# Where a kernel forms the sums of its weight blocks: the down projection's sums move from the input projection to the merge

## The chip, the cores and the metric

The kernel runs on one core of a Trainium2 chip. The metric is the device time of one execution in microseconds (us), the median of several runs. The profile comes from one further execution, recorded by the hardware profiler.

The engines are named as in the profile: PE is the matrix engine (PEld its weight loads), DVE the vector engine, ACT the scalar engine, POOL the GpSimd engine, SP the engine that does nothing but issue transfers (DMAs). SP, ACT and POOL each issue transfers in the order of their own instruction list; an issue that has to wait holds up the issues listed after it.

## The reference

One layer of a streaming encoder over 2048 + 64 = 2112 rows of width 1024, in float32:

- `proj = rmsnorm(x) @ w_in` with 5376 columns. From its parts come a gated causal convolution (branch A), an RWKV-7 recurrence over time with an 8-head matrix state (branch B) and 2048 gate columns.
- `m = sigmoid(gA) * (A @ w_conv_out) + sigmoid(gB) * (B @ w_rwkv_out)`, then `x += rmsnorm(m @ w_o)`. This is the merge.
- `x += rmsnorm((silu(h @ w_up_a) * (h @ w_up_b)) @ w_down)` with `h = rmsnorm(x)` and an inner width of 2816. These are the up and the down projection.

## The kernel before

**Stages.** Three follow one another. The input projection (`phase_a`) takes 160 weight blocks of 128 columns; each block is multiplied with two blocks of 264 rows, and one such product is a half unit, so that there are 320 half units. Three generators for the recurrence (`scan_prep`, `scan_solve`, `scan_chain`) are advanced between them. The merge (`merges`) goes three times, each time for two blocks of 352 rows, through `merge` (products with `w_ab`, gates multiplied in on DVE) and `merge_out` (products with `w_o`). The feed-forward stage (`ffn`) goes three times through the up and the down projection.

**Products.** A float32 operand is split into a high part (ACT) and a low part (DVE), and each product is three matmuls.

**Sums of weights.** The feed-forward products use a Strassen-like scheme of seven products of half-size blocks in place of eight. It needs four sums of the 2 x 2 blocks of each weight matrix. The kernel forms them itself: `weight_sums` loads the four blocks of a job into tiles named `sw` (four buffers), makes four additions on DVE in place (S_1, S_3, S_2, S_4) and writes the four results to scratch in memory, `us_s` for the up and `ds_s` for the down projection. There are 22 jobs for up (blocks of 128 x 512) and 12 for down (128 x 512, and 128 x 384 for every third). A job has four steps: loads; two additions; two additions; stores. Loads and stores are issued by SP. `sum_step` is called once per half unit and takes a step from half unit 24 on, every second time (`SUM_STEP = 2`): 136 steps. What is then left is written at the end of `projections`.

**Background work of the merge.** `self.bg` is a list of generators; `tick` advances each by one step. `merge` ticks twice after each of its 16 iterations, `merge_out` 16 times in all (32 in the third round), so there are 48, 48 and 64 ticks. In the list are the loads of the next round's operands (`merge_load`), the residual with its norm (`residual`, which adds on DVE into a tile `r`, stores it as `x1_s` from POOL, and loads the next one) and in the third round `norm_first`.

**Order.** The kernel gives each instruction a place in the written order only. The compiler's framework then lists the instructions of each engine in an order of its own, in which written order is a priority: an instruction whose operands and buffers are free can come long before its written place. Waits follow from the buffers: a load into a buffer waits until everything that used the buffer's last content is finished.

Of the kernel before, what the change touches and what calls it, by code (L numbers as in the profile page):

```python
# [9 lines left out]
F32 = mybir.dt.float32  # L10
# [3 lines left out]
ALU = mybir.AluOpType  # L14
AX = mybir.AxisListType

P = 128
# [12 lines left out]
NF = DFF // P  # L30
# [18 lines left out]
FB = T // 6  # L49
FH = NF // 2  # L50
HK = KT // 2
# [2 lines left out]

S_1, S_2, S_3, S_4 = range(4)

SUM_STEP = 2

DOWN = (("B11", "X", True), ("T2", "Y", False), ("B21", "X", False), ("D", "Y", False), ("T1", "Z", True), ("T4", "Y", False), ("B22", "Z", False))
UP = ("B11", "T1", "T2", "B21", "D", "B22", "T4")  # L60
# [4 lines left out]
KCHUNKS = ((0, 4), (4, 4), (8, 3))  # L65
# [20 lines left out]
class Trunk:  # L86
# [174 lines left out]
    def phase_a_setup(self, pool):  # L261
        nc = self.nc
        self.pa = pool
        self.pr_hist = pool.tile([P, 14], F32, name="pr_hist", bufs=1)
        nc.vector.memset(self.pr_hist, 0.0)
        self.u_hist = pool.tile([P, 4, 2], F32, name="u_hist", bufs=1)
        nc.vector.memset(self.u_hist, 0.0)
        self.pr_hist_s = pool.tile([P, 14], F32, name="pr_hist_s", bufs=1)
        nc.scalar.dma_start(out=self.pr_hist_s, in_=self.i["state_shift"])
        self.u_hist_s = pool.tile([P, 4, 2], F32, name="u_hist_s", bufs=1)  # L270
        nc.scalar.dma_start(out=self.u_hist_s, in_=self.i["state_conv"])
        self.hbufs, self.nb = 17, NB
        self.napply = self.sadd = nc.vector
        self.sq = "hf", 2
        self.later, self.parts, self.side = [], 0, []
        self.ready = 0
        self.summing, self.sum_wait = self.weight_sums(), 24
        self.lora_in, self.conv_u, self.kf, self.bn = {}, {}, {}, {}

    def project(self, w, h, n):  # L280
# [303 lines left out]
        for _ in self.summing:  # L584
            pass

    def weight_sums(self):

        nc = self.nc
        up, wd = self.i["w_up"], self.i["w_down"]  # L590
        jobs = [(lambda i, j, f=f: up[NF * i + f, :, HK * j:HK * j + HK, :], lambda s, f=f: self.us_s[s, f]) for f in range(NF)]
        for u in range(4):
            for k0, kn in KCHUNKS:
                jobs.append((lambda i, j, u=u, k0=k0, kn=kn: wd[2 * u + i, :, FH * j + k0:FH * j + k0 + kn, :],
                             lambda s, u=u, k0=k0, kn=kn: self.ds_s[s, u, :, k0 * P:(k0 + kn) * P]))
        for src, dst in jobs:
            w = {}
            for i in range(2):
                for j in range(2):
                    x = src(i, j)  # L600
                    w[i, j] = self.pa.tile([P, HK, P], F32, name="sw", bufs=4)[:, :x.shape[1]]
                    nc.sync.dma_start(out=w[i, j], in_=x)
            yield
            for n, (x, y) in enumerate((((1, 1), (1, 0)), ((1, 0), (0, 0)), ((0, 0), (1, 1)), ((0, 1), (0, 0)))):
                nc.vector.tensor_tensor(out=w[x], in0=w[x], in1=w[y], op=ALU.add)  # L605
                if n % 2:
                    yield
            for k, sm in (((1, 1), S_1), ((1, 0), S_3), ((0, 0), S_2), ((0, 1), S_4)):
                nc.sync.dma_start(out=dst(sm), in_=w[k].rearrange("p k c -> p (k c)"))
            yield  # L610

    def sum_step(self):
        self.sum_wait -= 1
        if self.sum_wait <= 0:
            self.sum_wait = SUM_STEP
            next(self.summing, None)
# [748 lines left out]
    def merges(self, th):  # L1365

        src, merged, last = [], [], []
        first = self.merge_load(0, src)
        next(first)
        self.fill(2)  # L1370
        for _ in first:
            pass
        self.fill()
        self.gates = self.gate_loads()
        self.gates_in = []
        for q in range(3):
            if q == 2:
                self.bg.append(self.norm_first(th, merged, last))
            ms = self.merge(q, src)
            src = []  # L1380
            if q < 2:
                self.bg.append(self.merge_load(q + 1, src))
            else:
                merged.append(True)
            self.bg.append(self.merge_out(q, ms))
        last.append(True)
# [98 lines left out]
```

## Time and profile before

| | |
|---|---|
| median of three runs | 3300.65 us (3297.57 to 3308.23) |
| profiled execution | 3302.73 us, span from first to last instruction 3301.0 us |
| mean granted PE clock | 0.975 of full speed |
| input projection | 0 to about 1510 us of the span |
| merge | about 1510 to 1900 us |
| feed-forward | about 1900 us to the end |
| DVE additions on `sw` | 136, the first at 24.7 us, the last at 1149.8 us |

A profile row of a group of instructions reads: line, engine, operation, destination <- source, shapes, count; then busy time and mean of one in ns; then the idle time of the engine before them and what ended it. PE is busy for 95% of the span, but a matmul at half the clock counts as busy too, so the granted clock has to be read beside it.

### The profile page before, as it was taken

To read this page: it belongs to the slowest core of one execution; us is meant where nothing else is said; L and a number is where in the kernel's file an instruction comes from. 1 tells how busy PE (TensorE), PEld (TensorE's weight loads), DVE (VectorE), ACT (ScalarE), POOL (GpSimd) and SP (SyncE) were. 2 spreads that over 40 slices of the span, in tenths; PEclk is the share of its full clock that TensorE was granted. 3 is DMA by queue.
4 is the path that set the end of the run, shared out by engine and by line. 5 is a ranking of instruction groups with operands and counts; after the bars stand their busy time and mean duration, and the time that the engine had idled before them with its cause. 6 is when DMAs were issued, how large, how long until landed. Compare 5 with 4: busy or idle time off the path is not lost.

```text
span 3301.0 us, 64364 instructions
## 1 busy us (share of the span) xinstructions
PE 3138.5 (95%) x23060; PEld 3061.5 (93%) x23060; DVE 2370.1 (72%) x5091; ACT 1734.6 (53%) x3418; POOL 493.7 (15%) x906
## 2 busy tenths in 40 slices
PE   6999999999989999998999999999999999999997
PEld 5889899889989999998999999999999999999997
DVE  6766777778778867655476877776767776766667
ACT  6534664564476445544434455556645466544464
POOL 2310123122014200000010011210011200111100
PEclk9999899999989999999999999999999999999999
DMA  8778767775676756546475467778767877766675
GB/s 267 244 246 246 231 197 235 224 221 168 208 223 184 218 159 176 140 146 227 131 225 159 152 209 240 241 244 263 234 214 229 266 246 237 235 191 189 189 253 167
DMA packets 526226, 699.53 MB, mean 212 GB/s; under 512 B 111136, under 2 KB 358496, under 8 KB 525904
## 3 DMA queue, kind: packets, MB, share of 16 engines
q1 hardware_dynamic: 468528, 592.67, 59.0%
q0 software_dynamic: 25456, 72.20, 5.9%
q10 hardware_dynamic: 31920, 30.54, 2.7%
q8 instruction: 181, 2.97, 0.4%
q14 instruction: 141, 1.16, 0.1%
HBM read 522.10 MB, written 173.12 MB: 211 GB/s over the span
## 4 chain that ended last, share of the span: by engine, by line
issue 42%; PE 23%; DVE 7%; POOL 5%; DMA 4%; ACT 2%; POOLq 0%; SPq 0%; ACTq 0%; DVEq 0%
PE mm L136 18%; POOL tp_s L1228 3%; PE pu L136 3%; PE gy L136 1%; DVE w_lo L150 1%; DVE ti L761 1%; POOL x_s L1087 1%; DVE tm L759 1%; POOL out_y L1087 1%; DMA w_raw<-in_w_in 1%; DMA x<-x_s 1%; DMA lo_s<-ks 0%; PE tr L140 0%; POOL nb_s L1172 0%; PE pa L136 0%
## 5 line engine op out<-in xcount | busy, mean ns | idle before, releaser
L136 PE MATMUL mm<-h_hi,w_hi 128*128 128x264 f32 (+1 forms) x5112 | 1591.9, 312 | 52.0 <-DVE f L1247 22.0
L136 PE MATMUL mm<-h_hi,w_lo 128*128 128x264 f32 (+1 forms) x5112 | 1564.8, 306 | 9.3 <-DVE w_lo L150 6.0
L136 PE MATMUL mm<-h_lo,w_hi 128*128 128x264 f32 (+1 forms) x5112 | 1566.1, 307 | 6.0 <-DVE h_lo L217 5.3
L136 PEld LDWEIGHTS mm<-h_hi,w_hi 128*128 128x128 f32 x5112 | 979.1, 192 | 77.3 <-DVE f L1247 25.9
L136 PEld LDWEIGHTS mm<-h_hi,w_lo 128*128 128x128 f32 x5112 | 980.2, 192 | 12.2 <-DVE w_lo L150 7.4
L136 PEld LDWEIGHTS mm<-h_lo,w_hi 128*128 128x128 f32 x5112 | 980.4, 192 | 11.0 <-DVE h_lo L217 6.7
L188 ACT CAST w_hi<-w_raw 128x512 fp32r<-128x512 f32 (+1 forms) x810 | 488.0, 608 | 537.4 <-PE mm L136 318.7
L189 DVE TENSOR_TENSOR w_lo<-w_raw,w_hi 128x512 fp32r<-128x512 f32 (+1 forms) x810 | 539.6, 673 | 259.9 <-ACT w_hi L188 253.2
L136 PE MATMUL mm<-t_hi,w_hi 128*128 128x352 f32 x1116 | 360.9, 323 | 1.0 <-ACT mm L1329 1.0
L136 PE MATMUL mm<-t_hi,w_lo 128*128 128x352 f32 x1116 | 358.2, 321 | 0.0
L136 PE MATMUL mm<-t_lo,w_hi 128*128 128x352 f32 x1116 | 358.1, 321 | 0.0
L150 DVE TENSOR_TENSOR w_lo<-w_raw,w_hi 128x1024 fp32r<-128x1024 f32 x168 | 206.0, 1227 | 106.8 <-ACT w_hi L149 98.2
L149 ACT CAST w_hi<-w_raw 128x1024 fp32r<-128x1024 f32 x168 | 175.9, 1048 | 141.9 <-PE mm L136 95.7
L1228 POOL DMA_DIRECT2D tp_s<-f x231 | 125.1, 542 | 578.7 <-DVE f L1247 339.7
L136 PEld LDWEIGHTS mm<-t_hi,w_hi 128*128 128x128 f32 x1116 | 209.4, 188 | 1.9 <-ACT mm L1329 1.5
L136 PEld LDWEIGHTS mm<-t_lo,w_hi 128*128 128x128 f32 x1116 | 209.8, 188 | 0.3
L136 PEld LDWEIGHTS mm<-t_hi,w_lo 128*128 128x128 f32 x1116 | 209.6, 188 | 0.0
L189 DVE TENSOR_TENSOR t_lo<-d,t_hi 128x352 fp32r<-128x352 f32 x198 | 97.1, 521 | 73.6 <-ACT t_hi L188 73.0
L188 ACT CAST t_hi<-d 128x352 fp32r<-128x352 f32 x198 | 91.3, 486 | 89.6 <-DMA d<-tp_s 82.7
L759 DVE TENSOR_TENSOR tm<-al,ti 128x60 f32<-128x60 f32 (+27 forms) x527 | 117.9, 224 | 8.9 <-DMA gt_s<-psv 1.1
L761 DVE TENSOR_TENSOR ti<-ti,tm 128x60 f32<-128x60 f32 (+27 forms) x527 | 117.6, 223 | 7.7
L605 DVE TENSOR_TENSOR sw<-sw 128x512 f32<-128x512 f32 (+1 forms) x136 | 93.4, 687 | 34.1 <-DMA sw<-in_w_up 29.5
(207 smaller groups left out, 3753.6 us busy)
## 6 DMA issues: line engine op xcount, KB each, us to landing
w_raw<-in_w_in SPq DMA_DIRECT2D x168, 512.0 KB, 4.3
w_raw<-us_s SPq DMA_DIRECT2D x264, 256.0 KB, 3.2
w_raw<-in_w_up SPq DMA_DIRECT2D x198, 256.0 KB, 3.1
tp_s<-f POOLq DMA_DIRECT2D x231, 176.0 KB, 3.6
d<-tp_s SPq DMA_DIRECT2D x105, 352.0 KB, 3.9
w_raw<-ds_s SPq DMA_DIRECT2D x96, 256.0 KB, 3.6
sw<-in_w_up SPq DMA_DIRECT2D x88, 256.0 KB, 4.6
us_s<-sw SPq DMA_DIRECT2D x88, 256.0 KB, 3.4
```

What stands on the lines that cost most here:

```text
L136: self.nc.tensor.matmul(out, lhsT, rhs, **kw)
L149: nc.scalar.copy(out=hi[:, :kt], in_=raw[:, :kt])
L150: nc.vector.tensor_tensor(out=lo[:, :kt], in0=raw[:, :kt], in1=hi[:, :kt].bitcast(F32), op=ALU.subtract)
L188: nc.scalar.copy(out=hi, in_=x)
L189: (eng or nc.vector).tensor_tensor(out=lo, in0=x, in1=hi.bitcast(F32), op=ALU.subtract)
L605: nc.vector.tensor_tensor(out=w[x], in0=w[x], in1=w[y], op=ALU.add)
L759: nc.vector.tensor_tensor(out=tv, in0=al[0:np_, u, u + 1:32].unsqueeze(1).broadcast_to([np_, k, m]), in1=ti[0:np_, 0:k, u:u + 1].broadcast ...
L761: nc.vector.tensor_tensor(out=tu, in0=tu, in1=tv, op=ALU.add)
L1087: (nc.sync if rows else nc.gpsimd).dma_start(out=dst[d, :, t0:t0 + n], in_=x)
L1228: nc.gpsimd.dma_start(out=self.tp_s[TP[op], i], in_=x)
```

## The change

The sums of the up projection begin at half unit 72 instead of 24 and take a step every third half unit, so one job in 12 half units (88 steps). The sums of the down projection leave the input projection. They become a background generator of the merge, put into `self.bg` before its first round: 24 jobs of at most two blocks of 128 columns for each of the four loads (128 x 256, and 128 x 128 for every sixth), 96 steps. They live in the tiles named `d` (two buffers, each with room for two blocks), which are otherwise used only by the down projection's operands. Their loads stay on SP; their stores are issued by POOL. For both, the loads are now issued in the order in which the additions use them.

```
-SUM_STEP = 2
+SUM_FIRST, SUM_STEP = 72, 3
+ADDS = (((1, 1), (1, 0), S_1), ((1, 0), (0, 0), S_3), ((0, 0), (1, 1), S_2), ((0, 1), (0, 0), S_4))
...
-        self.summing, self.sum_wait = self.weight_sums(), 24
+        self.summing, self.sum_wait = self.up_sums(), SUM_FIRST
...
+    def sums_of(self, load, queue, src, dst):
+        nc = self.nc
+        w = load(src)
+        yield
+        for n, (x, y, _) in enumerate(ADDS):
+            nc.vector.tensor_tensor(out=w[x], in0=w[x], in1=w[y], op=ALU.add)
+            if n % 2:
+                yield
+        for x, _, sm in ADDS:
+            queue.dma_start(out=dst(sm), in_=w[x])
+        yield
+    def up_sums(self):
+        up = self.i["w_up"]
+        def load(src):
+            w = {}
+            for i, j in ((1, 1), (1, 0), (0, 0), (0, 1)):
+                w[i, j] = self.pa.tile([P, HK, P], F32, name="sw", bufs=4)
+                self.nc.sync.dma_start(out=w[i, j], in_=src(i, j))
+            return w
+        for f in range(NF):
+            yield from self.sums_of(load, self.nc.sync, lambda i, j: up[NF * i + f, :, HK * j:HK * j + HK, :],
+                                    lambda s: self.us_s[s, f].rearrange("p (k c) -> p k c", c=P))
+    def down_sums(self):
+        wd = self.i["w_down"]
+        def load(src):
+            w = {}
+            for i in (1, 0):
+                t = self.bc.tile([P, 2, FB], F32, name="d", bufs=2)
                 for j in range(2):
                     x = src(i, j)
+                    w[i, j] = t[:, j, :x.shape[1] * P].rearrange("p (k c) -> p k c", c=P)
+                    self.nc.sync.dma_start(out=w[i, j], in_=x)
+            return w
+        for u in range(4):
+            for k0 in range(0, FH, 2):
+                k1 = min(k0 + 2, FH)
+                yield from self.sums_of(load, self.nc.gpsimd, lambda i, j: wd[2 * u + i, :, FH * j + k0:FH * j + k1, :],
+                                        lambda s: self.ds_s[s, u].rearrange("p (k c) -> p k c", c=P)[:, k0:k1, :])
...
         self.fill()
+        self.bg.append(self.down_sums())
         self.gates = self.gate_loads()
```

## Rows read from the trace of the kernel before

**Rows 1.** Busy time by stage: PE, PEld, DVE, ACT, POOL, PEclk, DMA share, GB/s.
```profile
0.00:600.00 600.00, 532.61 (x4399) 510.13 (x4400) 429.98 (x935) 316.89 (x614) 129.25 (x232) 0.94 0.75 237
600.00:1180.00 580.00, 551.56 (x4990) 525.18 (x4988) 470.94 (x1252) 334.12 (x672) 135.71 (x264) 0.96 0.68 204
1180.00:1510.00 330.00, 323.63 (x3021) 311.51 (x3019) 209.25 (x557) 167.56 (x288) 23.16 (x32) 1.00 0.52 151
1510.00:1582.00 72.00, 63.83 (x370) 61.91 (x371) 50.72 (x98) 28.55 (x58) 2.44 (x3) 0.91 0.81 263
1582.00:1643.00 61.00, 61.00 (x385) 61.00 (x385) 27.62 (x50) 29.95 (x63) 0.00 (x0) 1.00 0.41 129
1643.00:1710.00 67.00, 64.96 (x392) 63.96 (x391) 51.45 (x100) 18.32 (x34) 8.40 (x16) 0.97 0.62 190
1710.00:1775.00 65.00, 64.74 (x404) 64.21 (x403) 33.58 (x64) 32.53 (x70) 0.28 (x1) 1.00 0.50 162
1775.00:1842.00 67.00, 60.93 (x354) 58.59 (x353) 58.16 (x109) 22.70 (x46) 8.66 (x16) 0.96 0.71 219
```

**Rows 2.** SP's issues in the first 40 us: start us, duration us, instruction.
```profile
5.88 0.34 SPq L602 DMA_DIRECT2D sw<-in_w_up  x1
34.91 2.26 SPq L602 DMA_DIRECT2D sw<-in_w_up  x4
```

**Rows 3.** Weight blocks of the input projection split on ACT (L149), by window.
```profile
0.00:100.00 100.00, 9.40 (x9) 0.93 0.81 265
100.00:200.00 100.00, 15.68 (x15) 0.97 0.81 257
```

**Rows 4.** DVE groups, 600 to 1180 us, shapes apart: the additions of the down sums.
```profile
L605 DVE TENSOR_TENSOR sw<-sw 128x512 f32<-128x512 f32 x32 | 22.9, 716 | 0.1
L605 DVE TENSOR_TENSOR sw<-sw 128x384 f32<-128x384 f32 x16 | 9.9, 619 | 0.0
```

**Rows 5.** The chain that ended last, 600 to 1200 us: start us, us, what.
```profile
611.92 0.60 DVE sw L605
...
677.20 5.93 DMA ds_s<-sw
...
1133.92 1.57 DVE sw L605
```

**Rows 6.** Waits of SP, 600 to 1180 us: total us, times, longest.
```profile
SPq L602 <- DMA ds_s<-sw: 22.3, 15, 4.8
```

**Rows 7.** Waits of PE, 600 to 1180 us.
```profile
PE pa L136 <- DVE v L704: 10.9, 6, 2.4
...
PE mm L136 <- DVE sw L605: 3.2, 1, 3.2
```

**Rows 8.** Waits of DVE for the sums' loads, whole input projection.
```profile
DVE sw L605 <- DMA sw<-in_w_up: 29.5, 12, 5.6
```

**Rows 9.** DVE groups, 1510 to 1842 us: an addition of width 352.
```profile
L1033 DVE TENSOR_TENSOR f<-f,mm 128x352 f32<-128x352 f32 x44 | 22.6, 514 | 4.2 <-PE mm L136 3.5 <-DMA f<-gt_s 0.7
```

**Rows 10.** The chain in the second merge: one residual tile from addition to the next addition.
```profile
1656.54 0.45 DVE r L1086
1656.98 0.30 issue
1657.29 0.55 POOL x_s L1087
1657.83 0.91 issue
1658.75 3.52 DMA x_s<-r
1662.29 2.30 DMA r<-in_x
1664.61 0.05 DVEq L1086
```

**Rows 11.** Tile `r`, 1510 to 1900 us: its loads (first and last start), and DVE's wait.
```profile
L1072 SPq DMA_DIRECT2D r<-in_x x34: 327/333/934, 1557.8 to 1842.6; - x34
...
DMA r<-in_x: 17.2, 21
```

**Rows 12.** Waits of PE in the merge, 1510 to 1842 us.
```profile
PE mm L136 <- DVE f L1033: 5.0, 5, 1.9
```

More of the change, by code (lines that the diff above doesn't have):

```diff
@@ L585, in projections @@
             pass
-    def weight_sums(self):
+    def sums_of(self, load, queue, src, dst):
         nc = self.nc
[L590 to L596, printed above, removed]
-            w = {}
-            for i in range(2):
+        w = load(src)
[7 more added lines that the diff above has]
+        yield
@@ L599, in weight_sums @@
+    def down_sums(self):
[4 more added lines that the diff above has]
+                t = self.bc.tile([P, 2, FB], F32, name="d", bufs=2)
                 for j in range(2):
                     x = src(i, j)
[L601 to L607, printed above, removed]
@@ L608, in weight_sums @@
-            for k, sm in (((1, 1), S_1), ((1, 0), S_3), ((0, 0), S_2), ((0, 1), S_4)):
-                nc.sync.dma_start(out=dst(sm), in_=w[k].rearrange("p k c -> p (k c)"))
-            yield
+                    w[i, j] = t[:, j, :x.shape[1] * P].rearrange("p (k c) -> p k c", c=P)
[6 more added lines that the diff above has]
+                                        lambda s: self.ds_s[s, u].rearrange("p (k c) -> p k c", c=P)[:, k0:k1, :])
```

## The prediction

> **What bounds the kernel now.** I read the busy time by stage first, with the granted clock beside it, then the waits of PE and the chain that ended last inside the stages that the change touches. PE bounds every stage: in the three rounds of the merge that the change fills (1510 to 1775 us) it is busy for 61.0 of 61 us in one and 64.7 of 65 in another [rows 1]. What can be gained or lost is therefore PE's idle time and the time at a lower clock. From 600 to 1180 us, where the down sums run, PE is idle for 580 - 551.6 = 28.4 us and its clock averages 0.96, which is another 0.04 x 580 = 23 us of work time. From 1180 to 1510, with no sums, 6.4 us are idle in 330 and the clock is 1.00; but that stretch also has less recurrence work, so the difference is not the sums' alone [rows 1]. DVE, at 470.9 of 580 us, is the engine behind most waits: the two largest in which DVE releases PE are shown, and one of them, 3.2 us, is an addition of the sums itself [rows 7].
>
> The second thing to see is that written places do not bind. The sums are written from half unit 24 on. Two halves make a block, so that is after the twelfth block of the main loop and the two in front of it; only 9 blocks were split in the first 100 us and 15 in the next [rows 3], which puts half unit 24 beyond 100 us. Yet the first load of the sums is issued at 5.88 us and the second job's at 34.91 [rows 2]. The sums run ahead, in time that the engines' lists have free. The residual's loads show the same in the merge: the first is at 1557.8 us, in the first round, though it is written behind that round's products [rows 11].
>
> **The later start and the wider step.** Both lower the priority of the up sums, which had already been run long before their turn. They keep their 88 additions and 176 transfers, so I take 0 us for this. What hides it is the free time on DVE (600 - 430 = 170 us up to 600 us, [rows 1]). If they really waited for their place, DVE would be freer up to some 330 us (72 half units at 4.6 us, from 1500 us over 326), but five of the 88 steps would be written behind the last product: 320 calls, first step at call 72, every third, makes 83. The last job would then load, add and store across the seam, about 8 us by the loop in [rows 10]. Ends: 8 us gained, 8 lost.
>
> **The new order of loads.** The first addition now needs the first two loads, not the last two. DVE waited 29.5 us in 12 waits for these loads [rows 8], 2.5 us each. An issue takes about half a microsecond with its gap (2.26 us for four, [rows 2]), so one or two issues earlier saves up to 1 us per wait, 12 us of DVE; PE sees a part. Ends 0 and 6 us, taken 2, nearer the lower end, as PE's list shows one wait of 3.2 us on these additions in the later stretch and is mostly held by others.
>
> **The down sums leave the input projection.** Gone are 48 additions, 22.9 + 9.9 = 32.8 us of DVE [rows 4], 48 loads and 48 stores on SP, and SP's 22.3 us in 15 waits for a store of the sums before the next load [rows 6], behind which weight and recurrence transfers queue. How much of that was on the path? The chain from 600 to 1200 us has eleven pieces of an addition (0.60 the first, 1.57 the last; 6.5 us in all) and one wait for a store, 5.93 us [rows 5]: 12.4 us. Something else is late next: the 10.9 us in which PE waits for the recurrence's `v` [rows 7] stay. Ends: below, -3 us, since the lists are ordered anew and one wait like the 2.4 us of [rows 7] may come up again; above, 12.4 us and the clock that goes with it (23 us of clock per 28.4 us idle, so 12.4 x 1.8 = 22 us). I take 8, two thirds of the chain's pieces and no clock, since the clock's low spells need not be those of the sums.
>
> **They enter the merge.** There come 24 jobs, 80 additions of 256 and 16 of 128 elements. By the rows for 512 (716 ns) and 352 (514 ns) [rows 4, 9] an element costs 1.26 ns: estimated 393 and 232 ns, 31.4 + 3.7 = 35 us, 1.5 us a job. There are 96 loads and 96 stores of the same 23 MB as before in twice as many transfers.
>
> How fast can the jobs follow each other? Two `d` tiles make one job, so a job's loads wait for the last one's stores. The residual tile shows the loop: from the end of its addition 0.30 us, POOL's issue 0.55, landing 3.52, the next load 2.30 to 4.61 - without the 0.91 in which POOL waited for other work, 6.7 us [rows 10]. With four stores (3 x 0.55 more) and the additions (1.5) that is 9.9 us at least; at 10 to 11 us, 24 jobs take 240 to 264 us, and the two rounds with light or middling DVE load end at 1775, 265 us after the start. So they just fit before the third round, whose merge has DVE at 58.2 of 67 us [rows 1].
>
> DVE then goes from 50.7 to about 60 of 72 us in the first merge (six jobs), from 51.5 to 61 of 67 in the second, and stays under 60% in the two `merge_out` [rows 1]. The additions also wait for their loads in DVE's list, since the list is made before the transfers' true times are known: the residual's tile cost DVE 17.2 us in 21 waits [rows 11], 0.5 us for each of 34 loads. That adds 3 us per merge: 64 of 67 in the second, nearly full. PE hides lags of DVE through eight accumulators, two for an iteration of some 3.8 us (61 us over 16), so three iterations ahead; so far it waits 5.0 us for gate products in the whole merge [rows 12]. Ends: 0 (all in free time) and 35 us (all additions on the path). I take 4: one more such wait of 1 to 2 us per round and its clock, nearer the low end as three of the four stretches have a quarter of DVE or more left. The first merge's start is the other place: DMA share 0.81 at 263 GB/s there means 325 GB/s when full; six jobs of 0.96 MB are 5.8 MB, 18 us or 0.25 of the stretch, 1.06 together, 4 us too many. Ends 0 and 4; taken 1, since a job's loads are issued after the round's own.
>
> The stores moved to POOL could be thought to have a way of their own. POOL's store in [rows 10] lands in 3.52 us with 0.62 of DMA in use. The Trainium skill ("DMA: Bandwidth & Descriptors", section "Issuing engines are not separate DMA queues") says the reverse: transfers started by the scalar, sync or gpsimd engine run on the same 16 DMA engines and interleave, and starting them elsewhere saves only the sequencer's time. By that rule the 4 us above would be the term, by the unhurried landing it would be 0; no row here shows POOL's stores in a full stretch.
>
> **Sum.** -2 - 8 + 4 + 1 = -5 us against the profiled execution's 3302.73 us, 3297.7. That execution lies 2.1 us above the median of the runs shown, so the median to expect is 3295.6: 3296 us.
>
> **The rivals.** *The clock comes back with the sums.* If the stalls of [rows 5] started the low spells, the term of 8 is 22, with the loads' order at 4 and 5 for the merge: -21, or 3280 us. For it: the stretch without sums has clock 1.00 [rows 1]; against: less recurrence work there.
>
> *DVE fills up in the merge.* If the additions are listed too early, each job costs DVE not only its 1.5 us but a wait like those for `sw`, 2.5 us [rows 8]; and if eight jobs fall into each merge, as the written ticks have it (32 ticks, four steps), DVE needs 51.5 + 8 x 4 = 83 of 67 us in the second and 83 of 72 in the first [rows 1]: 16 + 11 = 27 us late, less the gain of 8: 3320 us, slower. It decides from about 1.1 us of wait per job at six jobs in the second merge ((67 - 51.5) / 6 - 1.5). For it: waits of 5.6 us happened [rows 8]; against: the residual's loop in the same stage costs 0.5 us a load [rows 11]. Its far end, with the whole 6.2 us of store, load and issue waited out each time, 2 x 8 x 7.7 - 15.5 - 21.3 = 86 us, needs an order as written, which [rows 2, 11] speak against.
>
> *Nothing on the path.* Something else held PE in [rows 5] just as late, and the merge hides the jobs: 3300 us, within 2.
>
> *The change does what it says and the up sums wait for their place*: 8 gained early, 8 lost at the seam; the same time as the forecast, so it gets no chance of its own.
>
> **How the numbers follow.** Forecast 0.34, clock 0.32, DVE full 0.25, nothing 0.09. What a measurement of this kernel can tell from no change is about 0.3%, 10 us: faster is below 3291, slower above 3310. The forecast's own range is 3286 to 3304, which gives 0.05 faster, 0.28 same, 0.01 slower; the clock case gives 0.30 faster and 0.02 same; the full DVE 0.22 slower and 0.03 same; nothing on the path 0.09 same. Together 0.35, 0.42 and 0.23. As both signs hold much, the range reaches to both outer cases, with 6 us beyond the one (both ends of the loads' order and of the clock) and 2 beyond the other: 3274 to 3322.
>
> **What would show it.** In the new profile: the first `sw` load still within the first 50 us, and the up sums' additions done long before 1500 us (else the later start binds); from 600 to 1180 us DVE about 33 us lighter, PE's idle time near 20 us rather than 28, no wait of SP for `ds_s`; additions on `d` from about 1515 to 1775 us, 10 to 11 us apart by jobs, PE still busy for over 95% of the second merge. It would be wrong if `d` additions reach far past 1800 us, if DVE's waits for the `d` loads exceed 1 us a job, or if the input projection ends at 1510 us as before.

## The result: the changed kernel is slower by 0.56%

| | before | after |
|---|---|---|
| median of 11 | 3303.31 us (3286.62 to 3310.06) | 3319.80 us (3310.70 to 3334.26) |
| ratio after/before, 95% interval | | 1.0056 [1.0037, 1.0075] |
| profiled execution | 3302.73 us, clock 0.975 | 3334.26 us, clock 0.972 |

The ratio is 18.5 us of 3303 [12, 25]. The forecast was 3296 us, so the time went the other way; it lies in the range, at the price of the rival in which DVE fills up. The profiled execution after is the longest of its 11: the profile shows a loss of 31.5 us where the medians show 16.5, so the stage times below make the loss look some 15 us larger than it usually is.

The stages can be cut at two places that both kernels have: the first gate product of the merge on DVE, and the first copy of the up projection's product on ACT. The views of these two lines, first of the kernel before (line, engine, operation and tile, count, ns min/median/max, first and last start in us, shape), then of the kernel after:

```profile
L1033 DVE TENSOR_TENSOR f<-f,mm x48: 506/514/522, 1533.9 to 1850.7; 128x352 f32<-128x352 f32 x48
...
L1257 ACT COPY f<-mm x66: 437/446/451, 1914.9 to 3125.2; 128x352 f32<-128x352 f32 x66
```

```profile
L1054 DVE TENSOR_TENSOR f<-f,mm x48: 505/512/521, 1518.4 to 1883.1; 128x352 f32<-128x352 f32 x48
...
L1278 ACT COPY f<-mm x66: 437/446/449, 1947.4 to 3157.0; 128x352 f32<-128x352 f32 x66
```

The merge begins 1533.9 - 1518.4 = 15.5 us earlier and lasts 1947.4 - 1518.4 = 429.0 us in place of 381.0. What follows takes 3332.5 - 1947.4 = 1385.1 us in place of 1386.1. So in these two executions 15.5 us were gained in the input projection and 48 lost in the merge. The merge between these two places, before and then after (columns as in [rows 1]):

```profile
1533.90:1914.90 381.00, 372.63 (x2281) 368.17 (x2280) 264.49 (x506) 157.93 (x327) 17.35 (x32) 0.99 0.56 175
```

```profile
1518.40:1947.40 429.00, 382.03 (x2276) 373.60 (x2275) 292.43 (x601) 154.02 (x326) 69.30 (x128) 0.94 0.67 209
```

PE's idle time grows from 8.4 to 47.0 us. The same products keep it busy 9.4 us longer, at a clock of 0.94 in place of 0.99.

Busy time by stage after, columns as in [rows 1]:

```profile
0.00:600.00 600.00, 540.20 (x4513) 517.83 (x4514) 446.82 (x967) 322.91 (x623) 128.91 (x232) 0.96 0.76 238
600.00:1180.00 580.00, 554.52 (x5046) 528.90 (x5046) 461.21 (x1229) 338.02 (x679) 120.47 (x267) 0.97 0.57 166
...
1510.00:1582.00 72.00, 63.93 (x393) 62.18 (x392) 46.32 (x103) 16.98 (x35) 13.01 (x24) 1.00 0.82 263
...
1643.00:1710.00 67.00, 49.23 (x290) 47.94 (x289) 44.12 (x87) 15.35 (x29) 14.95 (x28) 0.85 0.65 200
1710.00:1775.00 65.00, 55.54 (x314) 53.06 (x314) 46.15 (x102) 20.38 (x45) 15.16 (x28) 0.92 0.82 265
```

Look at 1643 to 1710: PE falls from 64.96 to 49.23 of 67 us and its clock from 0.97 to 0.85. DVE, which was given more to do in the merge, is less busy there than before, 44.12 us against 51.45 [rows 1], and the DMA share is 0.65 where it was 0.62. (The windows are cut by time, and the merge began 15.5 us earlier, so they do not hold quite the same work. Over the whole merge DVE is busy for 0.68 of the time against 0.69.) No engine is full; work is late.

Where the sums run now (views of the tiles `sw` and `d`):

```profile
L609 SPq DMA_DIRECT2D sw<-in_w_up x88: 327/422/3978, 13.8 to 475.3; - x88
L595 DVE TENSOR_TENSOR sw<-sw x88: 673/685/1247, 24.3 to 480.9; 128x512 f32<-128x512 f32 x88
...
L625 SPq DMA_DIRECT2D d<-in_w_down x96: 327/394/1567, 1518.4 to 1787.3; - x96
L595 DVE TENSOR_TENSOR d<-d x96: 283/424/427, 1522.8 to 1790.3; 128x256 f32<-128x256 f32 x80, 128x128 f32<-128x128 f32 x16
```

The up sums still run far ahead of their written place. Their last addition, at 480.9 us, even comes earlier than with the old start, step and order of loads (569.2 us in the kernel with the down sums alone moved, below). The down sums' 24 jobs take 269 us from first load to last, 11 us each.

The waits of the merge after, 1480 to 1960 us (engine, line, tile <- what it waited for: total us, times, longest):

```profile
DVE d L595 <- DMA d<-in_w_down: 76.9, 39, 5.9
...
PE mm L138 <- DVE acc L186: 21.4, 2, 17.6
PE mm L138 <- ACT h_hi L190: 11.5, 4, 6.0
PE mm L138 <- DVE f L1054: 8.8, 8, 1.9
...
SPq L625 <- DMA ds_s<-d: 83.3, 39, 6.4
```

DVE stands 76.9 us before additions on `d`, and SP 83.3 us before their loads. PE waits for gate products little more than in [rows 12]. Its longest wait, 17.6 us, is for `acc`, the sum of squares for the first round's norm, which is taken in the second merge. In the kernel before that wait was 3.1 us at most:

```profile
PE mm L136 <- DVE acc L184: 3.1, 1, 3.1
```

DVE's timeline ahead of the end of that wait shows why (start us, us, instruction; in brackets the idle time before it and what ended it):

```profile
1651.01 0.42 DVE L595 TENSOR_TENSOR d<-d 128x256 f32<-128x256 f32 x1 [4.51 <-DMA d<-in_w_down]
1651.35 0.52 DVE L186 TENSOR_TENSOR acc<-acc,e 128x352 f32<-128x352 f32 x1
...
1658.76 0.43 DVE L595 TENSOR_TENSOR d<-d 128x256 f32<-128x256 f32 x1 [3.35 <-DMA d<-in_w_down]
1659.10 0.52 DVE L186 TENSOR_TENSOR acc<-acc,e 128x352 f32<-128x352 f32 x1
...
1666.75 0.42 DVE L595 TENSOR_TENSOR d<-d 128x256 f32<-128x256 f32 x1 [3.81 <-DMA d<-in_w_down]
1667.54 0.89 DVE L595 TENSOR_TENSOR d<-d 128x256 f32<-128x256 f32 x2 [0.36 <-DMA d<-in_w_down]
1668.34 0.52 DVE L186 TENSOR_TENSOR acc<-acc,e 128x352 f32<-128x352 f32 x1
```

Each `acc` addition stands in DVE's list behind an addition on `d` that waits for its load, and runs the moment that one is done. So the chain of `acc` advances at the pace of the sums' loop, one or two for each job of some 8 us here; the addition at 1668.34 ends PE's wait at 1668.91. PE's next largest wait, for `h_hi`, leads to DVE too: ACT, which makes `h_hi`, waited longer for DVE's gate sums `f` than without down sums (69.6 us against 45.8 in the kernel below that has none):

```profile
ACT h_hi L190 <- DVE f L1056: 69.6, 20, 7.4
```

SP's timeline of the same stretch shows the loop's other half:

```profile
1647.18 1.95 SPq L625 DMA_DIRECT2D d<-in_w_down  x2
1649.23 0.38 SPq L933 DMA_DIRECT2D w_raw<-in_w_ab  x1
...
1656.04 2.07 SPq L625 DMA_DIRECT2D d<-in_w_down  x3
1658.22 0.37 SPq L933 DMA_DIRECT2D w_raw<-in_w_ab  x1
```

A load into `d` waits for a store of the last job, and the weight load listed next waits with it. That this costs PE time is not shown: between 1518 and 1947 us no engine waited for a load of `w_ab` or `w_o`, and ACT waited 22.7 us for loads of other operands (`x`), against 8.8 without down sums. The chain that ended last between 1500 and 1800 us runs mostly through POOL's stores of the sums (start us, us, what):

```profile
1525.89 0.54 POOL ds_s L599
1526.43 7.11 issue
1533.56 0.54 POOL ds_s L599
...
1544.33 0.55 POOL ds_s L599
```

From one job's first store to the next one's (1533.56 to 1544.33) are 10.8 us. For the piece called "issue" this view names no cause; POOL's timeline puts it down to waiting for DVE's next addition on `d` (7.12 us before the store at 1533.56). In that time the stores land and the next blocks are loaded and added.

### The profile page after: what moved, and what is told of

The parts are those of the page before. It is cut to its first block, busy times and chain, and to the rows that moved or that the text cites. A ratio compares the mean times of both kernels' runs of the same rounds, so it can differ in the third digit from the quotient of the medians.

```text
span 3332.5 us, 64681 instructions
## 1 busy us (share of the span) xinstructions
PE 3140.2 (94%) x23060; PEld 3060.4 (92%) x23060; DVE 2387.3 (72%) x5139; ACT 1728.1 (52%) x3418; POOL 529.8 (16%) x1002
## 4 chain that ended last, share of the span: by engine, by line
issue 41%; PE 23%; DVE 7%; POOL 6%; DMA 4%; ACT 1%; POOLq 0%; SPq 0%; DVEq 0%; ACTq 0%
PE mm L138 19%; POOL tp_s L1249 3%; PE pu L138 3%; POOL ds_s L599 1%; PE gy L138 1%; DVE w_lo L152 1%; DVE ti L782 1%; DVE tm L780 1%; DMA x<-x_s 1%; POOL x_s L1108 1%; POOL out_y L1108 1%; DMA nb_s<-x 0%; PE tr L142 0%; DVE hf L371 0%; DVE h_lo L219 0%
## 5 line engine op out<-in xcount | busy, mean ns | idle before, releaser
L1108 POOL DMA_DIRECT2D out_y<-r x40 | 21.6, 541 | 483.5 <-DVE r L1107 482.5
```

The source lines that it names most:

```text
L1108: (nc.sync if rows else nc.gpsimd).dma_start(out=dst[d, :, t0:t0 + n], in_=x)
```

## The experiments

Three explanations stand against each other. *DVE's additions*: it is the 38 us of work and the waits in DVE's list alone. *Traffic*: 23 MB more in the merge slow other transfers. *The loop in the lists*: addition, store, landing, load, addition goes round through one pair of `d` tiles, and whichever engine's list holds its waiting instructions delays what is listed behind them. Each ratio is to the kernel before, run on the same chip. Groups of kernels ran on different chips, so that a difference between two of these ratios is less sure than either.

For reading across, the stretch 1500 to 1900 us of each profile (input projection's end and the merge):

| kernel | ratio, 95% | PE busy of 400 us | clock | GB/s |
|---|---|---|---|---|
| before | 1 | 381.9 | 0.97 | 183 |
| after | 1.0056 [1.0037, 1.0075] | 350.2 | 0.92 | 225 |
| up sums alone changed | 0.9974 [0.9953, 0.9996] | 383.5 | 0.98 | 180 |
| down sums alone moved | 1.0099 [1.0071, 1.0126] | 349.8 | 0.92 | 227 |
| no down sums | 0.9908 [0.9880, 0.9937] | 389.0 | 0.99 | 180 |
| no additions | 1.0083 [1.0053, 1.0113] | 345.1 | 0.94 | 220 |
| loads on POOL, no additions | 1.0071 [1.0047, 1.0095] | 341.4 | 0.93 | 213 |
| all of the sums on POOL | 1.0192 [1.0165, 1.0218] | 306.2 | 0.87 | 203 |
| POOL holds the sums alone, no additions | 0.9939 [0.9913, 0.9966] | 381.1 | 0.98 | 231 |
| the same with additions, on POOL | 0.9953 [0.9935, 0.9971] | 377.6 | 0.98 | 230 |
| additions and loads paced | 0.9963 [0.9941, 0.9985] | 377.3 | 0.97 | 227 |

### The two parts of the change, and what there is to gain

The up sums alone changed (later start, wider step, order of loads). The down sums stay in the input projection, behind them, as 12 jobs on `sw` tiles (`down_sums_pa`), with the new order of loads too:

```
-        self.summing, self.sum_wait = self.up_sums(), SUM_FIRST
+        self.summing, self.sum_wait = self.all_sums(), SUM_FIRST
...
+    def all_sums(self):
+        yield from self.up_sums()
+        yield from self.down_sums_pa()
...
-        self.bg.append(self.down_sums())
```

> Only the first half of the change: up sums from half unit 72 every third half unit, loads in the new order; the down sums stay in the input projection as 12 jobs on `sw` tiles behind them. If the later start has no effect (my prediction's 0 us), the `sw` additions of the up sums still run within the first 500 us and the time is that of before, 3293 to 3310. If the loss of the change comes from the up sums' later start, it is near 3320. Merge stage as before, PE idle about 13 us from 1510 to 1900.

The down sums alone moved (up sums as before):

```
-SUM_FIRST, SUM_STEP = 72, 3
+SUM_FIRST, SUM_STEP = 24, 2
...
-            for i, j in ((1, 1), (1, 0), (0, 0), (0, 1)):
+            for i, j in ((0, 0), (0, 1), (1, 0), (1, 1)):
```

> Only the second half: down sums in the merge exactly as changed; up sums from half unit 24 every second half unit with the old order of loads. If the merge is the cause, the time is that of the changed kernel, 3312 to 3328, with DVE's waits for the `d` loads again at about 77 us and one PE wait for `acc` of over 10 us. If the later start of the up sums was part of it, 3300 to 3310.

No down sums at all:

```
-        self.bg.append(self.down_sums())
...
-                            yield self.ds_s[SUMS[op], u].rearrange("p (k c) -> p k c", c=P)[:, k0:k0 + kn, :]
+                            yield wd[2 * u, :, k0:k0 + kn, :]
```

> The changed kernel without the down sums anywhere (no loads, additions or stores of them; the down projection reads plain blocks in place of the four sums, the same number of bytes, so its output is another). It gives the floor: what the input projection gains when they leave. By the profiled runs the merge's first gate product came 15.5 us earlier (1518.4 against 1533.9) and the merge itself took 48 us longer; if that is right the time is about 3285 to 3291 and the merge 381 us from first gate product to the first up block. If the gain in the input projection was one run's chance, 3298 to 3306.

Measured 3292.10, 3335.72 and 3272.96 us, each outside what was expected: just under it, 8 us over it, 12 us under it. The loss belongs to the down sums in the merge: moved alone they cost 0.99%, with the same waits as in the changed kernel (76.4 us on DVE, 82.6 on SP, PE 18.0 for `acc` in two waits). The up sums' part gains 0.26% by itself. Taking the down sums away gains a further 0.9974 - 0.9908 = 0.66%, 22 us (some 10 to 34 by the two intervals); a kernel that only moves them should not come below this floor of 0.9908.

### Is it DVE's work, or the traffic?

The loads and stores stay, the additions go:

```
-            nc.vector.tensor_tensor(out=w[x], in0=w[x], in1=w[y], op=ALU.add)
+            if queue is not nc.gpsimd:
+                nc.vector.tensor_tensor(out=w[x], in0=w[x], in1=w[y], op=ALU.add)
```

> The changed kernel with all loads and stores of the down sums in the merge, but without their 96 additions (what is stored is the plain blocks, so the output is another). Theory A: the loss is DVE waiting in its list for the `d` loads (76.9 us in 39 waits) with everything behind it late; without additions DVE waits for nothing and the time falls to the floor, 3285 to 3293. Theory B: the loss is the transfers, 23 MB more in the merge and SP held 83.3 us by the stores before the next loads; then most of the loss stays, 3310 or more. Theory C, DVE's 35 us of work alone: between, about 3300, but then the next experiments with additions and no waits must stay there.

Measured 3330.56 us. With no addition on `d` anywhere the kernel is as slow as with them, so a loss of this size needs no addition. But it is not the same loss: PE's wait for `acc` is back at 3.7 us. The waiting moved. First DVE's timeline of this kernel, then SP's, then POOL's:

```profile
1642.37 0.52 DVE L1108 TENSOR_TENSOR r<-r,o 128x352 f32<-128x352 f32 x1
...
1652.68 0.51 DVE L1056 TENSOR_TENSOR f<-f,mm 128x352 f32<-128x352 f32 x1
1685.29 1.02 DVE L1108 TENSOR_TENSOR r<-r,o 128x352 f32<-128x352 f32 x2 [32.09 <-DMA r<-in_x]
```

```profile
1654.89 1.76 SPq L626 DMA_DIRECT2D d<-in_w_down  x4
...
1667.14 1.88 SPq L626 DMA_DIRECT2D d<-in_w_down  x4
...
1680.99 1.78 SPq L1094 DMA_DIRECT2D r<-in_x  x2
```

```profile
1678.78 1.14 POOL L1109 DMA_DIRECT2D x_s<-r  x2
```

The load of the residual's tile `r` is issued only at 1680.99 us. Two lists hold it up. In SP's it stands behind one job after another. In POOL's the store of the tile's last content, whose addition was done at 1642.9 us, stands behind the stores of the sums until 1678.78; the load waits for this store at the end, 0.9 us. DVE stands 32.09 us before its addition to `r`, and PE waits 34.4 us for a gate product listed behind it. SP's wait for the sums' stores is 85.6 us, as in the changed kernel.

So the loads were taken off SP too, and issued by POOL; once complete, once without additions:

```
-                    self.nc.sync.dma_start(out=w[i, j], in_=x)
+                    self.nc.gpsimd.dma_start(out=w[i, j], in_=x)
```

> The changed kernel, complete, with the loads of `d` issued by POOL. SP is free of the sums, DVE still has the additions, which still wait for loads that wait for stores. If SP's list was the whole cause, 3270 to 3290. If DVE's own waits for the `d` loads (76.9 us) are a cause of their own, DVE still waits for over 50 us, PE still waits over 10 us for `acc`, and the time stays at 3308 to 3325.

> As the kernel without the 96 additions (the stored sums are plain blocks, so the output is another), but the loads of `d` are issued by POOL as well, so that no load of the sums stands in SP's list. All 23 MB still move in the merge. Queue theory (SP's list is held by loads that wait for stores; in the kernel without additions that was 85.6 us of SP's time and one 32.1 us wait of DVE for `r`): SP is free, the merge runs as without sums, 3268 to 3285. Traffic theory (the transfers themselves slow the merge's other loads): stays at 3310 to 3335 as before.

And with the additions on POOL as well, which leaves nothing of the sums on DVE or SP:

```
-            nc.vector.tensor_tensor(out=w[x], in0=w[x], in1=w[y], op=ALU.add)
+            (nc.gpsimd if queue is nc.gpsimd else nc.vector).tensor_tensor(out=w[x], in0=w[x], in1=w[y], op=ALU.add)
```

> Loads, additions and stores of the down sums all on POOL, so that neither SP nor DVE has an instruction of the sums in its list. If the cause is that in-order lists of busy engines hold waiting instructions, this is the floor plus little: 3270 to 3288, the best of the complete kernels. Against it: the residual's stores are on POOL too and would now queue behind the sums; if that binds, DVE waits for `r` by more than the 18 us of before and the time is 3290 to 3310. A traffic theory expects 3310 or more.

Measured 3327.19 us (1.0095 [1.0074, 1.0117]; DVE waits 114.8 us for `d`), 3322.13 and 3360.14 us. All three slower, the last most of all. By the texts above 3322 and 3360 us speak for traffic; POOL's timeline without additions gives another reason:

```profile
1673.76 2.32 POOL L600 DMA_DIRECT2D ds_s<-d  x4 [0.52 <-DMA d<-in_w_down]
1677.03 2.27 POOL L626 DMA_DIRECT2D d<-in_w_down  x4 [0.95 <-DMA ds_s<-d]
1679.51 2.24 POOL L600 DMA_DIRECT2D ds_s<-d  x4 [0.20 <-issue]
1681.75 1.09 POOL L1109 DMA_DIRECT2D x_s<-r  x2
```

POOL also issues the residual's stores `x_s`, and these now stand behind a row of jobs: the additions of the two at 1681.75 were done at 1627.3 us. The next `r` load waits for such a store (SP 55.5 us at once), DVE for the load (54.1 us), PE for the gate product behind it (44.5 us). With the additions on POOL the same three waits are 91.9, 90.7 and 82.1 us.

One edit then takes the other stores out of that list. The merge's residual stores go to SP, the sums stay whole on POOL, without and with additions:

```
-                (nc.sync if rows else nc.gpsimd).dma_start(out=dst[d, :, t0:t0 + n], in_=x)
+                (nc.sync if rows or dst is self.x1_s else nc.gpsimd).dma_start(out=dst[d, :, t0:t0 + n], in_=x)
```

> The kernel with loads and stores of the down sums on POOL and no additions (output another), and now also the merge's residual stores moved from POOL to SP, so that POOL's list holds nothing but the sums. Theory as it now stands: whichever in-order list carries the sums' loop falls behind, and what is lost is the work listed behind it (in the run before, the residual's stores on POOL, one wait of DVE for `r` of 54 us). Then nothing is behind it now: 3268 to 3285, PE's longest wait in the merge under 6 us, although all 23 MB move. If the transfers themselves cost, 3300 or more.

> The complete kernel with loads, additions and stores of the down sums on POOL and the merge's residual stores on SP. By the list theory 3270 to 3288, faster than the kernel before by 0.3 to 0.8%, with DVE waiting for `r` under 40 us in all. If POOL's additions slow DVE's own by sharing memory, or the residual's stores now hold SP, 3288 to 3305. Traffic theory: 3310 or more.

Measured 3280.53 and 3284.98 us. Without additions the ratio goes from 1.0071 to 0.9939 by this line alone, and the traffic does not shrink. The stretch 1500 to 1900 us by windows, after and then this kernel (columns as in [rows 1]):

```profile
1500.00:1900.00 400.00, 350.20 (x2051) 340.92 (x2052) 271.25 (x561) 134.81 (x284) 69.30 (x128) 0.92 0.71 225
```

```profile
1500.00:1900.00 400.00, 381.10 (x2303) 375.53 (x2304) 266.98 (x513) 158.60 (x330) 100.24 (x185) 0.98 0.71 231
```

The same DMA share moves even more bytes, and PE is 30.9 us busier: the traffic theory falls as the main cause. What traffic may still cost lies within the 0.31% between this kernel and the one without down sums. The Trainium skill ("DMA: Bandwidth & Descriptors", section "Issuing engines are not separate DMA queues") says that starting transfers from several engines saves only the sequencer's time. That they share the 16 DMA engines agrees with the equal DMA share here; that only issue time is at stake does not: which list a store stands in decides between 1.0071 and 0.9939.

With the additions, on POOL, the sums are complete and the kernel has the lowest ratio of the complete ones: 0.9953 [0.9935, 0.9971], faster than before and after. In its merge no wait of PE passes 5 us, while the loop goes on waiting on POOL, where nothing is listed behind it that is needed soon:

```profile
PE mm L138 <- DVE f L1054: 10.0, 6, 3.0
...
POOL d L625 <- DMA ds_s<-d: 54.6, 32, 4.1
```

How much of this is the residual's stores alone? The same line in the kernel before and in the changed kernel:

> The kernel before with only the merge's residual stores on SP. If that move is neutral by itself, the time is that of before within 0.3%. If it is worth something (SP's store is issued sooner), 0.3 to 0.6% faster, and the gain of the all-POOL kernel is not the sums' place.

> The changed kernel with only the merge's residual stores on SP; loads of the sums still on SP, additions on DVE, stores on POOL. By the list theory SP and DVE are still held by the sums, so the loss stays: 0.4 to 1.0% slower than before. If the residual's stores were the trouble in the changed kernel too, it would be at or under the kernel before.

Measured 0.9982 [0.9964, 0.9999] (3291.68 us) and 1.0020 [1.0003, 1.0036] (3303.38 us). The move is worth 0.18% by itself and 0.36% in the changed kernel, more than expected, as 0.4 to 1.0% slower than before was to stay. That it is worth more there than by itself is not clear of the intervals. The waits of DVE for `d` (73.1 us), of SP for `ds_s` (83.6) and of PE for `acc` (16.7 at once) all stay, so they do not come from the residual's stores.

### Can the loop stay where it is?

Jobs of one block, so that the two `d` tiles hold two jobs in flight:

```
...
-            for k0 in range(0, FH, 2):
-                k1 = min(k0 + 2, FH)
+            for k0 in range(FH):
+                k1 = k0 + 1
```

> Queues as in the changed kernel (loads on SP, additions on DVE, stores on POOL), but 44 jobs of one block, each in one `d` tile, so that two jobs are in flight and a job's loads wait for the stores of the last but one. If the loop through one set of buffers is what holds the lists, the waits of SP for `ds_s` and of DVE for `d` fall well below 83 and 77 us and the time is 3285 to 3305, in spite of 176 additions in place of 96. If it is the number of instructions and transfers, it is slower than the changed kernel, 3330 or more.

Measured 3293.74 us, 0.9996 [0.9974, 1.0018]: the loss against the kernel before is gone, with SP's wait for `ds_s` down to 51.8 us, though DVE still waits 62.1 us for `d` and PE 9.6 us at once for `acc`.

The additions tied behind the last addition of the merge that is written before them (`issue_after` keeps an instruction behind a given one in its engine's list), and six ticks a job; then also the loads, behind the last weight load; then the first of these with jobs of one block, as two generators of 22 jobs each:

```
...
+            with self.tc.issue_after(self.mark):
+                for x, y, _ in ADDS:
+                    nc.vector.tensor_tensor(out=w[x], in0=w[x], in1=w[y], op=ALU.add)
...
+                    with self.tc.issue_after(self.mark_sp):
+                        self.nc.sync.dma_start(out=w[i, j], in_=x)
```

> The changed kernel (loads SP, additions DVE, stores POOL) with each job's four additions put in DVE's list behind the last merge addition written before them, four ticks after the loads, so that the list can't place them earlier than written; a job takes six ticks instead of four. If the early placing of additions on DVE is what makes DVE late, its waits for `d` fall from 77 to under 20 us and PE's wait for `acc` from 21 to under 6: 3280 to 3297. SP's loads can still be listed early and wait for stores: if that is the larger part, 3300 to 3320.

> As the last, and the loads of a job also stay behind the last weight load written before them in SP's list. If both lists matter, SP's waits for `ds_s` fall from 83 to under 25 us too, and this is the best kernel with the queues of the change: 3272 to 3290. If it is no faster than the one with only the additions held back, SP's part is nothing with additions paced.

> Queues of the change (loads SP, additions DVE, stores POOL), 44 jobs of one block, two in flight, additions held behind the last merge addition written before them, four ticks after their loads. If waits for the buffers and early additions are all there is, SP's waits for `ds_s` go under 25 us, DVE's for `d` under 15, PE's for `acc` under 6, and the ratio to before is 0.991 to 0.996. If the 176 additions of 0.29 us (51 us of DVE) cost by themselves, 0.997 or more.

Measured 3295.53 us (0.9972 [0.9955, 0.9989]), 3292.47 us (0.9963 [0.9941, 0.9985]) and 3295.18 us (0.9996 [0.9978, 1.0013]). The engines, instructions and bytes of the changed kernel, listed later and at a slower pace, gain where it lost; the additions now reach to 1883 us, and tie and pace were not separated. DVE's wait for `d` falls from 76.9 to this, in the kernel with both ties:

```profile
DVE d L600 <- DMA d<-in_w_down: 7.0, 5, 2.9
```

and PE's longest wait for `acc` from 17.6 to 8.4 us, where under 6 was expected. SP still waits 61.8 us for `ds_s`, where under 25 was expected, and the second tie gains nothing clear over the first (0.9963 against 0.9972). So a part of SP's list in the loss is not shown. Half-size jobs on top did not help: SP's wait stayed at 64.0 us, where less than 25 was expected, and 176 additions replace 96. That was a miss; why two jobs in flight don't shorten SP's wait there is open.

## Why the prediction was wrong

**Later start: right that the place does not bind, its value too small.** First load at 13.8 us, last addition at 480.9. The prediction gave 0 us to the later start and 2 to the order of loads; both together, with the down sums' loads in the new order too, measure 0.26%, 9 us [1, 16]. DVE's wait for these loads was 27.5 us in 11 waits in the input projection with the old start and order, and 20.0 in 13 with the new: 7.5 us of DVE, inside the 12 allowed. The 9 us lie above the term's end of 6, but their interval reaches below it. Which of the edits did it was not separated.

**Leaving the input projection: the sign right, the size open.** The forecast took 8 us, between -3 and 22. The ratios give 22 (some 10 to 34, from 0.66% between no down sums and the up part alone), the upper end, at which the rival of the returning clock stood. The traces give less: the first gate product comes at 1522.9 us with the up sums alone changed and at 1513.1 without down sums, 9.8 us. The clock did rise in the changed kernel, from 0.94 to 0.96 and from 0.96 to 0.97 in the two stretches [rows 1]. But it rose as far with the down sums still there, in the kernel with the up sums alone changed:

```profile
0.00:600.00 600.00, 537.75 (x4496) 515.35 (x4497) 449.17 (x967) 322.17 (x623) 128.96 (x232) 0.96 0.80 250
600.00:1180.00 580.00, 548.83 (x5034) 522.07 (x5033) 468.18 (x1266) 335.32 (x674) 124.65 (x266) 0.98 0.65 193
```

So the rival's mechanism, a clock that comes back because the down sums leave, is not what these rows show. DVE did not get 33 us lighter from 600 to 1180 us but 9.7, as other work took the place: 5046 matmuls ran there in place of 4990. PE's idle time there is 25.5 us, not near 20.

**Entering the merge: the step that failed.** It read: "I take 4: one more such wait of 1 to 2 us per round and its clock, nearer the low end as three of the four stretches have a quarter of DVE or more left", from 0.5 us of wait per load in the residual's loop, and 1 us for the DMA. The runs give 1.0056 - 0.9908 = 1.48%, 49 us (some 38 to 60 by the two intervals), in place of 5, beyond the bound of 35 us. The loop's own time was right (11 us a job, 38.4 us of additions for 35), and so was its end (1790 for 1775). What failed is the price of a wait: it was priced as DVE's time, which was to be had. But a wait in an in-order list is paid by what is listed behind it. The 76.9 us are 0.8 us for each of 96 loads and 3.2 us a job, three times the 1.1 us from which the rival was said to decide. In the changed kernel this was above all DVE's list: the additions to `acc` and the gate sums stood behind the additions on `d`, and with these tied behind the merge's own the ratio is 0.9972. The other lists were not costed. SP's 22.3 us of waits [rows 6] were counted as gone from the input projection, and not as coming back; they came back as 83.3 us in the merge, though what these cost PE is not shown. POOL's list, in which the residual's stores now stand with those of the sums, was named for its speed of landing alone; taking the residual's stores out of it gave back 0.36%.

**The rival with the right number** had DVE's list and the wait per job right (2.5 us taken, 3.2 measured) but expected DVE to fill up. It did not: in 1643 to 1710 us it is less busy than before, and over the merge its busy share is 0.68 against 0.69. Without additions on DVE the loss is as large, but it appears in another list: POOL's is shown by moving one store out of it, SP's was not separated. Its 3320 us agree with the median partly by chance: it took 27 - 8, the ratios give 49 - 22 - 9.

**The clock inside the loss.** In the 17.6 us wait PE does almost nothing; what follows begins at half speed. The windows around its end in the kernel after (columns as in [rows 1]):

```profile
1651.00:1668.90 17.90, 0.34 (x3) 0.05 (x1) 9.10 (x21) 4.49 (x8) 5.40 (x10) 0.57 0.63 202
1668.90:1673.70 4.80, 4.79 (x14) 4.29 (x15) 2.72 (x6) 1.04 (x2) 1.09 (x3) 0.50 0.64 201
```

The granted clock is 0.50, the 1.2 GHz level, for the 4.8 us behind the wait, which costs another 2.4 us of work.

**What stays open.** How the loss divides among the lists of SP, DVE and POOL in the changed kernel: the residual's stores and the tie with its slower pace each recover a part, and the parts may overlap. The best complete kernel stays 0.45% above the floor without down sums. Its lead over the kernel before is clear of the noise; over the up part alone (0.9974), over the residual stores alone (0.9982), or over the paced kernels (0.9963, 0.9972), it is not, as the intervals overlap. More `d` tiles were not tried.

## What to carry to other kernels

A background loop in which a load waits for the last job's store can cost more than its instructions: for each engine that issues a step of it, ask what stands behind the waiting instruction in that engine's list, and price the wait at that. Give such a loop a list of its own, and move what shares the list (here the residual's stores) elsewhere, or tie its steps behind work that has to run first. Where an engine is less busy after a change that gave it work, look for the wait at the head of its list, not for load.

## What the runs showed of the hardware

An addition of 128 x 256 on DVE took 422 ns in the changed kernel and one of 128 x 128 289 ns, against estimates of 393 and 232 from wider ones. The 128 elements between them cost 133 ns, so an estimated 156 ns do not go by the width, and narrow jobs cost more than their elements.

On POOL the 128 x 256 addition took 827 ns in the mean (782 with the residual's stores on POOL too). While POOL added, DVE's own additions of two ordinary tiles took longer: from 1500 to 1790 us those to `acc` took 699 ns, against 523 in the kernel in which POOL has the same loads and stores and no additions. The gate products, which read an accumulator of PE and one tile, did not: 513 ns against 515.

A transfer's issue on POOL took 542 ns in the median, against 394 on SP for the same loads in the changed kernel.
